# A YOCO-style decoder trunk on one core: rounding of activations at the entry of the recurrent stage, the first loads and filling products, and the end of W_o

## The chip, the cores and the metric

The kernel runs on one core of one Trainium2 chip. The metric is the device time of one execution in microseconds (us); the time of a kernel is the median of its runs. Three runs of the kernel before gave 1004.2, 1003.19 and 1003.34 us, median 1003.34 us.

## The reference, cut to what matters

256 tokens of width 1024 pass through two layers. Layer 0: a SwiGLU feed-forward (half step), a recurrent block (RG-LRU), a second feed-forward. Then keys, values and forget gates are computed once. Layer 1: feed-forward, attention, feed-forward. Every sub-layer has an RMSNorm before and after it. Cut down:

```
def swiglu(x, w_gate, w_up, w_down):
    return (silu(x @ w_gate) * (x @ w_up)) @ w_down

for layer in range(2):
    f = swiglu(rms_norm(h, ffn1_pre_g[layer]), ffn1 weights);  h = h + 0.5 * rms_norm(f, ffn1_post_g[layer])
    hn = rms_norm(h, mix_pre_g[layer])
    m = recurrent_block(hn, ...) if layer == 0 else forgetting_attention(hn, ...)
    h = h + rms_norm(m, mix_post_g[layer])
    f = swiglu(rms_norm(h, ffn2_pre_g[layer]), ffn2 weights);  h = h + 0.5 * rms_norm(f, ffn2_post_g[layer])
```

The recurrent block begins with `gx = x @ w_in` (1024 to 2 x 1344 columns), the attention ends with `o @ w_o`. All is float32.

## The kernel before, in words

**Products.** A float32 product is made of three products of rounded halves (`mm3`, L180 to L185): x and w are each split into an upper part (fp32r, `xhi`, `whi`) and a lower part (`xlo`, `wlo`, the remainder), and upper x upper, upper x lower, lower x upper are accumulated in PSUM. The activations, transposed, are the stationary side; 512 columns of weights stream.

**Tokens.** The 256 tokens are two halves, t=0 and t=1, of 128 rows. The weights stream from HBM in units of up to 128 x 1024 values (512 KB, tile `raw`, five buffers). `split` (L163) makes `whi` on ACT (L175) and `wlo` on DVE (L177), nine buffers each. A unit is used first for t=0, some slots later for t=1; one `slot` is the six products of one unit for one half. So a buffer comes free when t=1 is through with it.

**Order.** TensorE's order (PE) is written by hand: slots follow each other, and `defer(n, fn)` puts a piece of PE work n slots later. ACT, DVE and the DMA queues get their order from a scheduler with costs and priorities, except in the entry (below) and where an instruction is kept in program order. Engines take their instructions strictly in that order.

**Entry of the kernel** (L1083 to L1194, order by hand on all engines). x and the first four weight units are loaded in small pieces by one queue, SP: x's first half `h0` in pieces 0:2, 2:4, 4:8 (of 128 columns each), `h1` in 0:4, 4:8, the weights w0 and w1 in two halves each, w2 and w3 whole. In the text, h0[0:2] is such a piece and w0b the second half of w0. PE first runs filling products on a zeroed tile (`keep_busy`, L123), transposes the gains and x's tiles (`turn`), ACT rounds tile by tile straight from PSUM with the gain as scale (`x_up`), DVE makes the lower part (`x_lo`), and `products(t, i, "0uu ...")` runs the 512-column products of unit i: the digit is the half of the unit, the letters say which part of w and of x.

**Entry of the recurrent stage.** When the down projection of a half is finished, `enter` takes the sums of squares (ACT, L205), 1/rms on GpSimd (POOL, L198 and L200), and adds to h (DVE, L255 and L260). For the recurrent stage alone (`normed_x`) h is normalised again: squares of h in two pieces (ACT), 1/rms (POOL), `hn` (DVE, L285); five slots later PE transposes `hn` (L292), and `to_x` makes x: `xg = transposed * gain` (DVE, L222), `xhi` (ACT, L223), `xlo` (DVE, L228), each over 512 values. In the stage, eight units of the gate weights (called g0 to g7 here) are used for t=0 first, then for t=1.

**W_o.** `row_items` (L412) runs a projection with two PSUM banks per half. The last `rows` units of a half are kept back and run bank by bank, so that bank 0 ends before bank 1 and its squares can start. For t=0 of W_o that means: slot 7 of 8 (k=6) issues nothing on PE, slot 8 issues twelve products. The attention steps of t=1 (logits, exp on ACT, transposes, values) lie between these slots.

Of the kernel before, what the change touches and what calls it, by code (L numbers as in the profile page):

```python
# [9 lines left out]
F32 = mybir.dt.float32  # L10
F32R = mybir.dt.float32r
BF16 = mybir.dt.bfloat16
# [4 lines left out]
P = 128  # L17
D = 1024
# [26 lines left out]
def trunk_kernel(ctx: ExitStack, tc: tile.TileContext, A: dict, out: bass.AP):  # L45
# [19 lines left out]
    def gtbank():  # L65
        return psum.tile([P, 512], F32, tag="gt", name=nm("gt"), bufs=2)
# [14 lines left out]
    def defer(n, fn):  # L81
        pend.append([n, fn])
# [22 lines left out]

    h = [hpool.tile([P, D], F32, tag=f"h{t}", name=f"h{t}") for t in range(2)]

    def load_h(t, a, b):

        nc.sync.dma_start(h[t][:, a * P:b * P], A["x"][0, t * P:(t + 1) * P, a * P:b * P])  # L110
# [3 lines left out]
    idle = spool.tile([P, D], BF16, tag="junk", name="idle", bufs=1)  # L114
    nc.vector.memset(idle[:, :512], 0.0)
# [7 lines left out]
    def keep_busy(n):  # L123

        ps = trbank()
        for _ in range(n):
            nc.tensor.matmul(ps, idle[:, :P], idle[:, :512], start=True, stop=True)

    gT = cpool.tile([P, 56], F32, name="gT")

# [14 lines left out]
    def main_dest(gi, t):  # L145
        return (gi, xhi[:, :, t * P:(t + 1) * P], xlo[:, :, t * P:(t + 1) * P])
# [19 lines left out]
    def split(rawv, parts, n, pieces=1, dve=False):  # L166
        u = Unit()
        hi = wpool.tile([P, 1024], F32R, tag="whi", name=nm("whi"), bufs=WB)
        lo = wpool.tile([P, 1024], F32R, tag="wlo", name=nm("wlo"), bufs=WB)
        m = n // pieces  # L170
        for c in range(0, n, m):
            if dve:
                nc.vector.tensor_copy(hi[:parts, c:c + m], rawv[:, c:c + m])
            else:
                nc.scalar.activation(hi[:parts, c:c + m], rawv[:, c:c + m], AF.Copy)  # L175
            low = nc.gpsimd if dve else nc.vector
            low.tensor_tensor(lo[:parts, c:c + m], rawv[:, c:c + m], hi[:parts, c:c + m].bitcast(F32), ALU.subtract)  # L177
        u.hi, u.lo = hi[:parts, :n], lo[:parts, :n]
        return u
# [57 lines left out]
    rs = [None, None]  # L237

    def stat(t):
        ss = new_ss()  # L240
# [3 lines left out]
    def enter(t, dests, pf, gb, half, last=False, normed=False):  # L244

        f = 1.0 / 16 if half else 1.0 / 32
        ss = new_ss()
        t1 = []
        urgent = tc.high_priority()
        urgent.__enter__()  # L250
        for n in range(2):
            square_sum(pf[n], ss[:, n:n + 1], f)
        for n in range(2):
            t1.append(hpool.tile([P, 512], F32, tag="t1", name=nm("t1"), bufs=2))
            nc.vector.tensor_tensor(t1[n], pf[n], gb[:, n * 512:(n + 1) * 512], ALU.mult)  # L255
        r = rstd_of(ss, 2, f)
        m = 256 if last else 512
        for c in range(0, D, m):
            hn = h[t][:, c:c + m]
            nc.vector.scalar_tensor_tensor(hn, t1[c // 512][:, c % 512:c % 512 + m], r[:, 0:1], hn, ALU.mult, ALU.add)  # L260
            if last:
                nc.sync.dma_start(out[0, t * P:(t + 1) * P, c:c + m], hn)
        urgent.__exit__(None, None, None)
        if last:
            return

        def inputs():
            tps = [to_tp(h[t], n) for n in range(2)]
            for dest in dests:
                to_x(tps, dest)  # L270
            stat(t)

        def norm():
            with tc.high_priority():
                normed_x()

        def normed_x():
            ss = new_ss()
            for n in range(2):
                square_sum(h[t][:, n * 512:(n + 1) * 512], ss[:, n:n + 1])  # L280
            rs[t] = rstd_of(ss, 2)
            hn = []
            for n in range(2):
                hn.append(hpool.tile([P, 512], F32, tag="t1", name=nm("hn"), bufs=2))
                nc.vector.tensor_scalar(hn[n], h[t][:, n * 512:(n + 1) * 512], rs[t][:, 0:1], None, ALU.mult)  # L285

            def go():
                tps = []
                for n in range(2):
                    tp = gtbank()  # L290
                    for j in range(4):
                        nc.tensor.transpose(tp[:, j * P:(j + 1) * P], hn[n][:, j * P:(j + 1) * P], ident)  # L292
                    tps.append(tp)
                to_x(tps, dests[0])
            defer(5, go)

        if normed:
            norm()
        else:
            defer(3, inputs)  # L300

# [110 lines left out]
    def row_items(w, widths, get_x, post, rows=2, dve=False):  # L412

        acc = {}
        kept = [[], []]
        nk = len(widths)
        r0 = 0
        for k, kp in enumerate(widths):  # L420
            def prep(kp=kp, r0=r0, k=k):
                return split(load_raw(w[r0:r0 + kp, :], kp, D), kp, D, dve=dve and k % 2 == 1)

            def work(t, u, k=k):
                if k == 0:
                    acc[t] = [mmbank(), mmbank()]
                m = rows if t == 1 else min(rows, 2)
                if k >= nk - m:
                    kept[t].append((k, u))
                    if k < nk - 1:  # L430
                        return
                    todo = [(kk, uu, n) for n in range(2) for (kk, uu) in kept[t]]
                else:
                    todo = [(k, u, n) for n in range(2)]
                for (kk, uu, n) in todo:
                    mm3(acc[t][n], *get_x(t, kk), uu.hi[:, n * 512:(n + 1) * 512], uu.lo[:, n * 512:(n + 1) * 512],
                        kk == 0, kk == nk - 1)
                if k == nk - 1:
                    post(t, acc[t])
            items.append((prep, work))  # L440
            r0 += kp
# [624 lines left out]
    row_items(A["attn_w_o"][0], [P] * 8, lambda t, k: (att["oh"][t][:, k, :], att["ol"][t][:, k, :]),  # L1066
              lambda t, accs: enter(t, [main_dest(GI[("ffn2", 1)], t)], accs, gbox["mix1"], False), dve=True)
    ahead(n_q + 2, load_gb("mix1", A["mix_post_g"][1]))
    n_att = len(items)

# [13 lines left out]
    begin.__enter__()  # L1084
    raws = [new_raw() for _ in range(OPEN)]

    def load_w(i, a, b):

        nc.sync.dma_start(raws[i][:, a * 512:b * 512].rearrange("p (k n) -> p k n", k=b - a),
                          A["ffn1_w_gate"][0, (2 * i + a) * P:(2 * i + b) * P, :512].rearrange("(k p) n -> p k n", p=P))  # L1090
# [24 lines left out]

    tps = {}

    def turn(t, a, b):

        n = a // 4  # L1120
        if (t, n) not in tps:
            tps[t, n] = gtbank()
        for k in range(a, b):
            nc.tensor.transpose(tps[t, n][:, k % 4 * P:(k % 4 + 1) * P], h[t][:, k * P:(k + 1) * P], ident)

    def x_up(t, a, b):
        for k in range(a, b):
            nc.scalar.activation(xhi[:, k, t * P:(t + 1) * P], tps[t, k // 4][:, k % 4 * P:(k % 4 + 1) * P], AF.Copy,
                                 scale=gT[:, k:k + 1])

    def x_lo(t, a, b):
        for k in range(a, b):
            nc.vector.scalar_tensor_tensor(xlo[:, k, t * P:(t + 1) * P], tps[t, k // 4][:, k % 4 * P:(k % 4 + 1) * P],
                                           gT[:, k:k + 1], xhi[:, k, t * P:(t + 1) * P].bitcast(F32),
                                           ALU.mult, ALU.subtract)

    def products(t, i, order):

        for c in order.split():
# [3 lines left out]
            nc.tensor.matmul(first_acc[t], main_x(t, k)[c[2] == "l"], parts[i][c[1] == "l"][:, j * 512:(j + 1) * 512],  # L1143
                             start=k == 0 and c[1:] == "uu", stop=k == 7 and c == order.split()[-1])

    first_acc.extend(mmbank() for _ in range(2))
# [24 lines left out]
    x_up(1, 2, 4)  # L1171
    w_lo(1, 1, 2)
    products(0, 1, "0uu 0lu 1uu 0ul 1ul")
    turn(0, 4, 8)
# [6 lines left out]
    turn(1, 4, 8)  # L1181
    x_lo(0, 4, 8)
    products(0, 2, "0uu 1uu 0lu 1lu 0ul 1ul")
    x_up(1, 4, 8)
# [108 lines left out]
```

## Time and profile before

| | |
|---|---|
| runs of the kernel | 1004.2, 1003.19, 1003.34 us; median 1003.34 us |
| the profiled execution | 1004.31 us |
| its span, first to last instruction | 1002.6 us, so 1.71 us lie around it |
| mean granted TensorE clock | 0.999 |
| busy time | PE 993.2, weight loads 830.3, DVE 614.2, ACT 530.6, POOL 59.4 us |
| data moved | 178.88 MB, mean 178 GB/s |

The page gives busy time by engine, the span in 40 slices, and the chain of work that ended last. The timeline lists instructions in order of time: start in us, duration in us, engine, line, operation, output and input tiles, count, and in brackets the idle time of the engine before it and what released it. Matmuls are pipelined: the step from one start to the next, not the duration, is what one costs. PEld is the load of the stationary side, SPq and ACTq are the issuing of DMAs by the sequencers of SP and ACT.

### The profile page before, as it was taken

To read this page: it belongs to the slowest core of one execution; us is meant where nothing else is said; L and a number is where in the kernel's file an instruction comes from. 1 tells how busy PE (TensorE), PEld (TensorE's weight loads), DVE (VectorE), ACT (ScalarE), POOL (GpSimd) and SP (SyncE) were. 2 spreads that over 40 slices of the span, in tenths; PEclk is the share of its full clock that TensorE was granted. 3 is DMA by queue.
4 is the path that set the end of the run, shared out by engine and by line. 5 is a ranking of instruction groups with operands and counts; after the bars stand their busy time and mean duration, and the time that the engine had idled before them with its cause. 6 is when DMAs were issued, how large, how long until landed. Compare 5 with 4: busy or idle time off the path is not lost.

```text
span 1002.6 us, 12917 instructions
## 1 busy us (share of the span) xinstructions
PE 993.2 (99%) x4790; PEld 830.3 (83%) x4790; DVE 614.2 (61%) x768; ACT 530.6 (53%) x737; POOL 59.4 (6%) x98
## 2 busy tenths in 40 slices
PE   9999999999999999999999999999999999999997
PEld 6888888889988888888898888888888888888885
DVE  6656554668998555554686655554487475555542
ACT  6645443559986544443564444444466565444431
POOL 2400000100004000000100000000033000000000
PEclk9999999999999999999999999999999999999999
DMA  7867555565336766555467566555554067665531
GB/s 275 297 207 205 189 189 188 166 180 154 109 108 223 215 183 190 188 189 189 123 209 231 177 189 188 182 180 191 162 170 168 7 204 210 189 188 189 188 106 42
DMA packets 92788, 178.88 MB, mean 178 GB/s; under 512 B 11982, under 2 KB 32886, under 8 KB 92726
## 3 DMA queue, kind: packets, MB, share of 16 engines
q1 hardware_dynamic: 91862, 177.94, 55.9%
q8 instruction: 37, 0.61, 0.3%
q0 software_dynamic: 832, 0.12, 0.1%
q14 instruction: 25, 0.20, 0.1%
q10 hardware_dynamic: 32, 0.01, 0.0%
HBM read 176.95 MB, written 1.05 MB: 178 GB/s over the span
## 4 chain that ended last, share of the span: by engine, by line
PE 97%; DVE 1%; ACT 1%; issue 1%; POOL 0%; POOLq 0%; DVEq 0%; ACTq 0%
PE mm L183 28%; PE mm L185 28%; PE mm L184 28%; PE tr L481 2%; PE gt L709 2%; PE mm L1143 1%; PE mm L1027 1%; PE gt L1000 1%; PE mm L190 1%; PE mm L192 1%; PE mm L191 1%; PE gt L214 1%; PE tr L1016 1%; ACT junk L205 0%; PE tr L896 0%
## 5 line engine op out<-in xcount | busy, mean ns | idle before, releaser
L177 DVE TENSOR_TENSOR wlo<-raw,whi 128x1024 fp32r<-128x1024 f32 (+4 forms) x325 | 391.7, 1210 | 270.9 <-ACT whi L175 269.0
L175 ACT ACTIVATE whi<-raw 128x1024 fp32r<-128x1024 f32 (+4 forms) x325 | 338.1, 1045 | 315.6 <-PE mm L185 253.3
L183 PE MATMUL mm<-whi,xhi 128*128 128x512 f32 (+2 forms) x768 | 304.2, 396 | 0.0
L185 PE MATMUL mm<-whi,xlo 128*128 128x512 f32 (+2 forms) x768 | 298.7, 389 | 0.0
L184 PE MATMUL mm<-wlo,xhi 128*128 128x512 f32 (+2 forms) x768 | 298.0, 388 | 0.0
L185 PEld LDWEIGHTS mm<-whi,xlo 128*128 128x128 f32 x768 | 144.2, 188 | 30.5 <-DVE xlo L228 0.3
L184 PEld LDWEIGHTS mm<-wlo,xhi 128*128 128x128 f32 x768 | 144.5, 188 | 28.0 <-DVE wlo L177 0.3
L183 PEld LDWEIGHTS mm<-whi,xhi 128*128 128x128 f32 x768 | 144.3, 188 | 27.5
L183 PE MATMUL mm<-whi,hhi 128*128 128x512 f32 x352 | 139.1, 395 | 0.0
L185 PE MATMUL mm<-whi,hlo 128*128 128x512 f32 x352 | 137.8, 391 | 0.0
L184 PE MATMUL mm<-wlo,hhi 128*128 128x512 f32 x352 | 136.9, 389 | 0.0
L185 PEld LDWEIGHTS mm<-whi,hlo 128*128 128x128 f32 x352 | 66.1, 188 | 15.0
L184 PEld LDWEIGHTS mm<-wlo,hhi 128*128 128x128 f32 x352 | 66.1, 188 | 14.1
L183 PEld LDWEIGHTS mm<-whi,hhi 128*128 128x128 f32 x352 | 66.2, 188 | 13.0
L198 POOL TENSOR_SCALAR nv<-ss 128x1 f32<-128x1 f32 x24 | 12.0, 501 | 884.7 <-ACT junk L205 884.7
L475 DVE SCALAR_TENSOR_TENSOR prod<-mm,rstd,sil 128x512 f32<-128x512 f32 (+1 forms) x48 | 33.9, 706 | 38.0 <-PE mm L185 34.3
L466 ACT ACTIVATE sil<-mm,rstd 128x512 f32<-128x512 f32 (+1 forms) x48 | 31.2, 651 | 40.7 <-PE mm L185 40.7
L485 ACT ACTIVATE hhi<-tr 128x512 fp32r<-128x512 f32 (+1 forms) x48 | 26.6, 555 | 16.0 <-PE tr L481 15.9
L255 DVE TENSOR_TENSOR t<-mm,gb 128x512 f32<-128x512 f32 x24 | 16.3, 689 | 28.7 <-ACT junk L205 28.7
L205 ACT ACTIVATE junk<-mm 128x512 bf16<-128x512 f32 x24 | 14.2, 591 | 32.8 <-PE mm L185 32.8
L486 DVE TENSOR_TENSOR hlo<-tr,hhi 128x512 fp32r<-128x512 f32 (+1 forms) x48 | 30.5, 642 | 1.4
L183 PE MATMUL mm<-whi,zhi 128*128 128x340 f32 (+2 forms) x80 | 28.3, 354 | 0.0
(187 smaller groups left out, 935.6 us busy)
## 6 DMA issues: line engine op xcount, KB each, us to landing
raw<-in_ffn_w_down_dram SPq DMA_DIRECT2D x88, 512.0 KB
raw<-in_ffn_w_up_dram SPq DMA_DIRECT2D x80, 512.0 KB
raw<-in_ffn_w_gate_dram SPq DMA_DIRECT2D x78, 512.0 KB
raw<-in_rg_w_in_dram SPq DMA_DIRECT2D x20, 504.0 KB
raw<-in_ffn_w_gate_dram SPq DMA_DIRECT2D x20, 256.0 KB
raw<-in_rg_w_out_dram SPq DMA_DIRECT2D x10, 504.0 KB
raw<-in_ffn_w_up_dram SPq DMA_DIRECT2D x16, 256.0 KB
raw<-in_w_kv_dram SPq DMA_DIRECT2D x8, 512.0 KB
```

The costliest lines, as they stand in the source:

```text
L175: nc.scalar.activation(hi[:parts, c:c + m], rawv[:, c:c + m], AF.Copy)
L177: low.tensor_tensor(lo[:parts, c:c + m], rawv[:, c:c + m], hi[:parts, c:c + m].bitcast(F32), ALU.subtract)
L183: nc.tensor.matmul(ps, xh, wh, start=first, stop=False)
L184: nc.tensor.matmul(ps, xh, wl, start=False, stop=False)
L185: nc.tensor.matmul(ps, xl, wh, start=False, stop=last)
L255: nc.vector.tensor_tensor(t1[n], pf[n], gb[:, n * 512:(n + 1) * 512], ALU.mult)
L466: nc.scalar.activation(s[:, :nn], ps, AF.Silu, scale=rs[t][:, 0:1])
L475: nc.vector.scalar_tensor_tensor(pr[:, :nn], ps, rs[t][:, 0:1], s, ALU.mult, ALU.mult)
L481: nc.tensor.transpose(tp[:, j * P:(j + 1) * P], pr[:, j * P:(j + 1) * P], ident)
L485: nc.scalar.activation(hv, tp[:, :nn], AF.Copy)
L486: nc.vector.tensor_tensor(lv, tp[:, :nn], hv.bitcast(F32), ALU.subtract)
L709: nc.tensor.matmul(ps[:w, j * S:(j + 1) * S], wv[:, o:o + w], xc[:w, k, :], start=k == 0, stop=k == m - 1)
```

## The change

The entry: the second half of w0, `h1[0:4]` and the second half of w1 are issued on ACT's queue instead of SP's. The filling products read a constant tile that exists before the kernel starts, not a tile that DVE zeroes first; there are six and three of them instead of five and two. The first two tiles of x go to two PSUM banks, the others to banks of other kinds. In the order, `1uu` is put ahead of `0lu`, and the transposes of h0[2:4] go from before `0lu` to after `1lu`.

The entry of the recurrent stage: the transposes come six slots after `norm` instead of five. `to_x_tiles` takes x per 128-column tile straight from PSUM: eight ACT instructions with the gain as scale, eight DVE instructions, instead of two each of L222, L223 and L228. The first `whi` that is split after `norm` is kept in program order (`settled`), and so comes after the squares of h on ACT.

The end of W_o, t=0: one unit is kept back instead of two (`rows0=1`), so slot k=6 has its six products and slot k=7 six. For t=1, and for all other users of `row_items`, nothing changes.

```
     def keep_busy(n):
         for _ in range(n):
-            nc.tensor.matmul(ps, idle[:, :P], idle[:, :512], start=True, stop=True)
+            nc.tensor.matmul(ps, nc.const_aps.tensor(1.0, (P, P), BF16), nc.const_aps.tensor(1.0, (P, 512), BF16),
+                             start=True, stop=True)
...
-                nc.scalar.activation(hi[:parts, c:c + m], rawv[:, c:c + m], AF.Copy)
+                up = nc.scalar.activation(hi[:parts, c:c + m], rawv[:, c:c + m], AF.Copy)
+                if settled[0]:
+                    tc.keep_in_program_order(up)
+                    settled[0] = False
...
+    def to_x_tiles(tps, dest):
+        gi, xh, xl = dest
+        def operands(k):
+            return tps[k // 4][:, k % 4 * P:(k % 4 + 1) * P], gT[:, gi + k:gi + k + 1]
+        with tc.high_priority():
+            for k in range(8):
+                src, g = operands(k)
+                nc.scalar.activation(xh[:, k, :], src, AF.Copy, scale=g)
+            for k in range(8):
+                src, g = operands(k)
+                nc.vector.scalar_tensor_tensor(xl[:, k, :], src, g, xh[:, k, :].bitcast(F32), ALU.mult, ALU.subtract)
...
-                to_x(tps, dests[0])
-            defer(5, go)
+                to_x_tiles(tps, dests[0])
+            defer(6, go)
...
-                m = rows if t == 1 else min(rows, 2)
+                m = rows if t == 1 else rows0
...
     load_h(0, 0, 2)
     load_w(0, 0, 1)
+    load_w(0, 1, 2, nc.scalar)
     load_h(0, 2, 4)
-    load_w(0, 1, 2)
-    load_h(1, 0, 4)
+    load_h(1, 0, 4, nc.scalar)
     load_w(1, 0, 1)
-    load_w(1, 1, 2)
+    load_w(1, 1, 2, nc.scalar)
...
-    keep_busy(5)
+    keep_busy(6)
     gains_T(grow0, 16, 0)
-    turn(0, 0, 2)
-    keep_busy(2)
+    turn(0, 0, 1, gtbank())
+    turn(0, 1, 2, gtbank())
+    keep_busy(3)
...
-    products(0, 0, "0uu 0ul")
-    turn(0, 2, 4)
-    products(0, 0, "0lu 1uu 1ul")
-    turn(1, 0, 4)
+    products(0, 0, "0uu 0ul 1uu 0lu 1ul")
+    turn(1, 0, 2, early[0])
+    turn(1, 2, 4, trbank())
     products(0, 0, "1lu")
+    turn(0, 2, 4, early[1])
```

In the changed program's order, ACT's queue holds: the load of the gains, the table load, one small activation, then the three new loads. The third of them, w1's second half, waits for the semaphore of h0[0:2]. At the entry of the recurrent stage DVE's order for t=0 is: the two additions to h, both `hn`, five `wlo` (L177), four `xlo`, one product with the gain of t=1 (L255), three `xlo`, L255, the two additions to h of t=1, the last `xlo`. ACT's order there is: two squares of the sum, two squares of h, five `whi`, eight `xhi`.

More of the change, by code (lines that the diff above doesn't have):

```diff
@@ L1116, in trunk_kernel, with turn @@
     tps = {}
[L1118 to L1122, printed above, removed]
+    def turn(t, a, b, bank):
         for k in range(a, b):
-            nc.tensor.transpose(tps[t, n][:, k % 4 * P:(k % 4 + 1) * P], h[t][:, k * P:(k + 1) * P], ident)
+            tps[t, k] = bank[:, (k - a) * P:(k - a + 1) * P]
+            nc.tensor.transpose(tps[t, k], h[t][:, k * P:(k + 1) * P], ident)
     def x_up(t, a, b):
         for k in range(a, b):
-            nc.scalar.activation(xhi[:, k, t * P:(t + 1) * P], tps[t, k // 4][:, k % 4 * P:(k % 4 + 1) * P], AF.Copy,
+            nc.scalar.activation(xhi[:, k, t * P:(t + 1) * P], tps[t, k], AF.Copy,
                                  scale=gT[:, k:k + 1])
@@ L1144, in products @@
                              start=k == 0 and c[1:] == "uu", stop=k == 7 and c == order.split()[-1])
+    early = [mmbank() for _ in range(2)]
     first_acc.extend(mmbank() for _ in range(2))
-    keep_busy(5)
+    keep_busy(6)
     gains_T(grow0, 16, 0)
-    turn(0, 0, 2)
-    keep_busy(2)
+    turn(0, 0, 1, gtbank())
+    turn(0, 1, 2, gtbank())
+    keep_busy(3)
     x_up(0, 0, 2)
```

22 lines of the change are left out of this document (11 added, 11 removed).

## Prediction

> **What bounds the kernel now.** I read the page first, then the waits of the weight-load side of TensorE, then the timeline at the three places that the change touches. From the page:
>
> ```profile
> span 1002.6 us, 12917 instructions
> PE 993.2 (99%) x4790; PEld 830.3 (83%) x4790; DVE 614.2 (61%) x768; ACT 530.6 (53%) x737; POOL 59.4 (6%) x98
> PE 97%; DVE 1%; ACT 1%; issue 1%; POOL 0%; POOLq 0%; DVEq 0%; ACTq 0%
> ```
>
> PE is the chain from end to end. The change takes no product away (it adds two fillers), so it can only win where PE stands still or runs slowly. Where it stands still, the waits of its weight loads say (total us, times, longest):
>
> ```profile
> PEld mm L1143 <- ACT xhi L1128: 1.0, 2, 0.5
> PEld mm L1027 <- ACT pT L1018: 0.8, 2, 0.5
> PEld gt L292 <- DVE hn L285: 0.6, 1, 0.6
> ```
>
> L1143 is the entry, L292 the entry of the recurrent stage, L1027 the attention beside W_o. These three are among the longest of that view and hold 2.4 us. So the whole question is about 2 to 4 us in 1003, and 0.2% (2.0 us) is about what a measurement of this kernel can tell from no change.
>
> **A. Entry.** The rows of the stretch:
>
> ```profile
> 0.92 0.27 DVE L115 MEMSET idle<- 128x256 uint32 x1 [0.92 <-PEq L1278]
> 1.24 1.28 ACT L121 ACT_TABLE_LOAD   x1 [1.24 <-PEq L1278]
> 1.25 2.32 PE L127 MATMUL tr<-idle 128*128 128x512 bf16 x5 [1.25 <-DVE idle L115]
> 2.17 0.43 SPq L1089 DMA_DIRECT2D raw<-in_ffn_w_gate_dram  x1
> 2.65 0.43 SPq L110 DMA_DIRECT2D h<-in_x_dram  x1
> 6.34 0.63 ACT L1110 ACTIVATE whi<-raw 128x512 fp32r<-128x512 f32 x1 [1.28 <-DMA raw<-in_ffn_w_gate_dram]
> 7.27 0.63 PE L1143 MATMUL mm<-whi,xhi 128*128 128x512 f32 x1
> 7.70 0.63 PE L1143 MATMUL mm<-whi,xlo 128*128 128x512 f32 x1
> 8.00 0.78 PEld L1124 LDWEIGHTS gt<-ident,h 128*128 128x128 f32 x4 [0.39 <-DMA h<-in_x_dram]
> 10.51 0.40 PE L1143 MATMUL mm<-whi,xhi 128*128 128x512 f32 x1
> 10.74 0.40 PE L1143 MATMUL mm<-wlo,xhi 128*128 128x512 f32 x1
> 4.80:10.20 5.40, 4.41 (x7) 2.33 (x8) 1.00 0.89 312
> ```
>
> Two things cost here. First the pitch: products start 0.43 us apart at 7.27 and 7.70, 0.23 apart at 10.51 and 10.74, although the last row (L1143 alone: busy time and count of products on PE and of their weight loads, then granted clock, DMA share, GB/s) shows the granted clock at 1.00. It has seven products in 5.4 us. At the later pitch they would take 7 x 0.23 = 1.6; the slow pitch costs 7 x 0.20 = 1.4, and the rest, 2.4, is transposes and waiting for loads: w0b until 6.34, `h1[0:4]` until 8.00, then its rounding.
>
> The loads: w0b's issue moves from 2.17 to about 1.25 if ACT's queue goes on beside the table load, or back to 2.5 (1.24 + 1.28) if it waits for that; `h1[0:4]` from 2.65 to 1.7, or 3.0. Bounds for the gain of `h1[0:4]`: 0.95 us if issuing sets it, below nothing (-0.5) if ACT's queue is late. w0b was used 4.2 us after its issue and `h1[0:4]` 5.3 after, so each waits for others' bytes; I take half, 0.5 us. That `xhi` now needs only the first two transposes of t=1 saves two at 0.2 (four load in 0.78 at 8.00); the two of h0[2:4], now ahead of t=1's products, cost the same. The third filler costs nothing as long as PE waits for w0b behind it (0.43 if it doesn't). So 0.5.
>
> The pitch: fillers start when PE does, not behind DVE's 0.27 us memset, 0.3 us earlier, and nine of them instead of seven reach without a gap to about 5.5. If denser work brings the faster pitch sooner, each product ahead of 10.2 wins 0.20. Bounds: 0 (it changes at the same time) and 1.4 (all seven); the waits for loads take the place of most of it, so I take 0.3. **A = -0.8, from +0.5 (ACT's queue late) to -2.0 (0.95 and three quarters of 1.4).** Nothing behind eats it: from 10.2 to 20.7 ACT is busy 8.8 and DVE 9.0 of 10.5 us, so up to 1.5 us pass through.
>
> ```profile
> 10.20:20.70 10.50, 10.50 (x50) 8.45 (x49) 9.03 (x20) 8.78 (x19) 0.30 (x1) 1.00 0.82 286
> 17.25 2.02 ACT L175 ACTIVATE whi<-raw 128x1024 fp32r<-128x1024 f32 x2
> ```
>
> SP's load of the fifth unit now waits for w1's first half instead of w0b, so it is issued later; ACT rounds that unit at 17.25, which hides it.
>
> **B. Entry of the recurrent stage.**
>
> ```profile
> 185.62 0.30 POOL L198 TENSOR_SCALAR nv<-ss 128x1 f32<-128x1 f32 x1 [147.85 <-ACT junk L205]
> 188.09 1.03 ACT L175 ACTIVATE whi<-raw 128x1008 fp32r<-128x1008 f32 x1
> 189.03 0.61 ACT L205 ACTIVATE junk<-h 128x512 bf16<-128x512 f32 x1
> 189.83 0.70 POOL L198 TENSOR_SCALAR nv<-ss 128x1 f32<-128x1 f32 x1 [3.25 <-ACT junk L205]
> 191.15 0.39 PE L185 MATMUL mm<-whi,hlo 128*128 128x512 f32 x1
> 191.21 0.88 DVE L285 TENSOR_SCALAR hn<-h,rstd 128x512 f32<-128x512 f32 x2 [0.84 <-POOL rstd L200]
> 191.75 1.09 PE L292 MATMUL gt<-ident,hn 128*128 128x128 f32 x8 [0.22 <-DVE hn L285]
> 192.60 0.47 PE L183 MATMUL mm<-whi,hhi 128*128 128x512 f32 x1
> 196.81 0.39 PE L183 MATMUL mm<-whi,xhi 128*128 128x504 f32 x1
> 197.30 0.50 PE L185 MATMUL mm<-whi,xlo 128*128 128x504 f32 x1
> 203.58 0.40 PE L185 MATMUL mm<-whi,xlo 128*128 128x504 f32 x1
> 204.44 1.06 PE L292 MATMUL gt<-ident,hn 128*128 128x128 f32 x8 [0.47 <-DVE hn L285]
> 205.26 0.47 PE L183 MATMUL mm<-whi,xhi 128*128 128x504 f32 x1
> 801.14 0.39 PE L185 MATMUL mm<-whi,ol 128*128 128x512 f32 x1
> 802.16 0.48 PE L183 MATMUL mm<-whi,oh 128*128 128x512 f32 x1
> ```
>
> Between the last two rows lie eight transposes without a wait (L214): 1.02 us from the product before to the product after. Here it is 191.15 to 192.60 = 1.45 and 203.58 to 205.26 = 1.68: 0.43 and 0.66 us of standstill. A first `xlo` that comes late (197.30: 0.50 instead of 0.39) adds 0.11. Together 1.2.
>
> After: without the `whi` of 188.09 ahead of it the second square starts with its h, near 188.1, instead of 189.03. POOL's first step starts 0.8 later (189.83), and lasts 0.30 as at 185.62, not 0.70, as no `wlo` is running on DVE; `hn` starts 0.68 after its end: 189.9, ending 190.8. The transposes come six products (1.37 us) later, at 191.38 + 1.37 = 192.75. Both waits go. What is late next is DVE: five `wlo` now stand between `hn` and the first `xlo`. At 1.18 each (192.00 has two in 2.32) they end at 190.8 + 5.9 = 196.7; `xlo` of a tile takes 0.285 (14.40 has four in 1.13), ready at 196.95. PE goes on at 193.55, has twelve products until 196.3 and wants that `xlo` two products on, at 196.75: a new wait of 0.2, longer by whatever `hn` is late. `xhi` is no limit: five `whi` from 188.85, some 1.03 each, end at 194.0, and the tiles follow at 0.285 (13.22 has four in 1.14). The last `xlo` stands behind h of t=1: 0.1 more. **B = -1.2 + 0.3 = -0.9**; from -1.2 (no new wait) to 0 (the new wait as long as the old ones).
>
> ```profile
> 192.00 2.32 DVE L177 TENSOR_TENSOR wlo<-raw,whi 128x1008 fp32r<-128x1008 f32 x2
> 13.22 1.14 ACT L1128 ACTIVATE xhi<-gt,gT 128x128 fp32r<-128x128 f32 x4 [0.67 <-PE gt L1124]
> 14.40 1.13 DVE L1133 SCALAR_TENSOR_TENSOR xlo<-gt,gT,xhi 128x128 fp32r<-128x128 f32 x4 [0.54 <-ACT xhi L1128]
> ```
>
> **C. W_o.**
>
> ```profile
> 789.53 0.60 PE L1039 MATMUL tr<-ident,ot 128*128 128x128 f32 x4
> 790.44 1.10 PE L1027 MATMUL mm<-v,pT 128*128 128x64 f32 x8 [0.31 <-ACT pT L1018]
> ```
>
> Eight transposes took 0.8 above (1.02 less a product), so these four take 0.4 and the values could follow at 789.93; they wait for `pT` until 790.44: 0.5 us. After, six products (1.37 us) stand between and cover it. The first product behind transposes lasts 0.47 (192.60) instead of 0.39, and one such start is added: 0.1. The step after keeps six products between its transposes and its values, as all other steps have, and none of those waits. The sum of bank 0 ends 3 instead of 6 products before the slot's end, but the whole slot is 0.6 earlier. **C = -0.4**, from -0.6 to 0.
>
> **Sum.** -0.8 - 0.9 - 0.4 = -2.1. Against the profiled execution's own 1004.31 (span 1002.6 and 1.71 around it) that is 1002.2; that execution stands 0.97 above the median of the runs, which I carry over: 1003.34 - 2.1 = **1001.2**, 0.21% less.
>
> **Rivals.**
>
> 1. *The second queue moves only the issuing.* For: the data moved at 312 GB/s with the DMA engines 0.89 busy between 4.8 and 10.2, and w0b took 4.2 us from issue to use. Against: the first microseconds are not full. Then w0b and `h1[0:4]` land when they did, the third filler and the reordered transposes show, and A is +0.1 instead of -0.8: -1.2, **1002.1**. The Trainium skill, "DMA: Bandwidth & Descriptors", section "Issuing engines are not separate DMA queues", says just this: DMAs started by several engines run on the same 16 DMA engines and interleave, and starting them from several saves only the sequencer's time. By that rule this rival is the forecast.
> 2. *The pitch changes early.* If denser fillers bring the 0.23 us pitch at about 6.8 and loads come 0.95 earlier too, A is -2.0: -3.3, **1000.0**. For: the runs of the same kernel differ by 1.0 us, as much as five products' slow pitch. Against: the profile before had seven fillers and still changed its pitch only between 7.70 and 10.51. The Trainium skill, "TensorE: Matmul & The Clock Gate", Part 1, "What's actually happening", has the array at half clock until a free-running window of about 3.4 us was busy; the two pitches agree with it, the granted clock of 1.00 does not show it.
> 3. *DVE's five `wlo` cost what was won*: if `hn` ends at 191.7 instead of 190.8, as late as before less 0.4, the first `xlo` is 1.1 us late and B is 0: -1.2, **1002.1**. For: DVE takes its instructions in order and stands idle until `hn`. Against: the two squares lose the `whi` between them, which alone is 0.9.
> 4. *Slower: ACT's queue starts after the table load.* w0b lands after 6.9, PE stands still behind the fillers for over 1 us, and the faster pitch comes only after the products of unit 1 and the first six of unit 2: 18 x 0.20 = 3.6, and 0.4 for the loads. A is +4.0: +2.7, **1006.0**. It decides from w0b landing later than 6.9. Against: the queue of a sequencer and its engine are shown apart in the trace.
> 5. *The change doesn't do what it says*: in the changed order the waits' causes are in fact moved, so I give this no case of its own; C at 0 is within the range.
>
> **How the numbers follow.** Forecast 0.42, own range 1000.5 to 1002.0; rival 1 0.24, rival 2 0.18, rival 3 0.10, rival 4 0.06. The boundary of 0.2% is 1001.33, just above the forecast, which so gives 0.27 to faster and 0.15 to same; rival 2 is faster; rivals 1 and 3 are same but for 0.03; rival 4 is slower. Faster 0.48, same 0.46, slower 0.06. The range goes from 999.8 to 1002.9: rivals 1 to 3 with half a microsecond around them.
>
> **What would show it.** A: ACTq issues near 1.25, w0b's `whi` before 6.34, the 0.23 pitch before 10. B: no idle time before the transposes of `hn`; a PE wait of 0.2 to 0.3 on `xlo` at the first product of g0. C: no wait on `pT` there. The prediction is wrong if the products of unit 1 start later than before, or if PE waits more than 1 us on `xlo`.

## The result and the profile after

| | before | after |
|---|---|---|
| median of the runs | 1003.29 us (17 runs, 1002.9 to 1004.2) | 1001.38 us (17 runs, 1000.82 to 1002.81) |
| the profiled execution | 1004.31 us | 1001.1 us |
| ratio after to before | | 0.998, 95% interval 0.9972 to 0.9987 |

The changed kernel is 1.9 us faster at the median, the forecast was 1001.2. The two profiled executions differ by more, 3.2 us; that difference turns out to be the main point below.

The page after. PE is still the chain from end to end, and is busy 2.2 us less than before:

```profile
span 999.4 us, 12928 instructions
PE 991.0 (99%) x4792; PEld 829.4 (83%) x4792; DVE 613.0 (61%) x775; ACT 532.7 (53%) x749; POOL 59.0 (6%) x98
```

The waits of its weight loads (total us, times, longest). The rows of before for `xhi` at the entry (1.0), `hn` (0.6) and the longer one for `pT` are gone; what is left of B is one wait of a weight load for `xlo` (0.3, of which the products lose 0.1, as the rows of B show). The wait for `pT` that is left was there before, as the shorter of two:

```profile
PEld mm L187 <- DVE xlo L251: 0.3, 1, 0.3
PEld mm L1045 <- ACT pT L1036: 0.3, 1, 0.3
```

**A.** The timeline of the entry after. Both queues issue side by side, ACT's beside the table load. But w0a, which was rounded at 4.18 before, comes at 5.63, and PE stands still for it; from the second product on, though, products start 0.23 apart unless PE waits or transposes between them:

```profile
1.24 1.28 ACT L119 ACT_TABLE_LOAD   x1 [1.24 <-PEq L1296]
1.31 0.37 ACTq L1107 DMA_DIRECT2D raw<-in_ffn_w_gate_dram  x1
...
5.63 0.43 DVE L1126 CAST whi<-raw 128x512 fp32r<-128x512 f32 x1 [1.65 <-DMA raw<-in_ffn_w_gate_dram]
5.82 0.63 ACT L1128 ACTIVATE whi<-raw 128x512 fp32r<-128x512 f32 x1 [0.98 <-DMA raw<-in_ffn_w_gate_dram]
...
6.20 0.47 PE L1159 MATMUL mm<-whi,xhi 128*128 128x512 f32 x1 [0.57 <-DVE whi L1126]
6.51 0.39 PE L1159 MATMUL mm<-whi,xlo 128*128 128x512 f32 x1
...
19.26 0.40 PE L185 MATMUL mm<-whi,xhi 128*128 128x512 f32 x1
```

The same rows of before, w0a's rounding, the first product and the first regular product:

```profile
4.18 0.43 DVE L1108 CAST whi<-raw 128x512 fp32r<-128x512 f32 x1 [0.19 <-DMA raw<-in_ffn_w_gate_dram]
4.85 0.82 PE L1143 MATMUL mm<-whi,xhi 128*128 128x512 f32 x1
20.72 0.39 PE L183 MATMUL mm<-whi,xhi 128*128 128x512 f32 x1
```

The first regular product is the first one behind the hand-ordered entry. The busy times of the entry's products alone from 4.8 to 10.2 (PE, weight loads, granted clock, DMA share, GB/s) hold fourteen products where before held seven:

```profile
4.80:10.20 5.40, 3.80 (x14) 2.50 (x14) 1.00 1.01 362
```

**B.** The eight transposes of `hn` follow the products without a wait, for both halves; only the first product with `xlo` is stretched, 0.33 us to the next start instead of 0.23:

```profile
188.56 0.88 DVE L302 TENSOR_SCALAR hn<-h,rstd 128x512 f32<-128x512 f32 x2 [1.99 <-POOL rstd L202]
189.36 5.68 DVE L179 TENSOR_TENSOR wlo<-raw,whi 128x1008 fp32r<-128x1008 f32 x5
191.28 1.04 PE L309 MATMUL gt<-ident,hn 128*128 128x128 f32 x8
195.36 0.49 PE L187 MATMUL mm<-whi,xlo 128*128 128x504 f32 x1
195.69 0.39 PE L185 MATMUL mm<-whi,xhi 128*128 128x504 f32 x1
203.25 1.04 PE L309 MATMUL gt<-ident,hn 128*128 128x128 f32 x8
222.28 3.62 PE L727 MATMUL gt<-xc,gw 126*126 126x256 f32 x16
```

**C.** Six products stand between the transposes of `ot` and the values, which no longer wait:

```profile
786.96 0.60 PE L1057 MATMUL tr<-ident,ot 128*128 128x128 f32 x4
787.31 0.48 PE L185 MATMUL mm<-whi,oh 128*128 128x512 f32 x1
...
788.79 1.00 PE L1045 MATMUL mm<-v,pT 128*128 128x64 f32 x8
992.00 0.40 PE L187 MATMUL mm<-whi,hlo 128*128 128x512 f32 x1
```

The last row is the last product of the kernel. Between such fixed points the time can be split: the first regular product (end of the entry), the first gate product `gt<-xc,gw` (222.28 here), the transposes of `ot` (786.96), the last product. Before they stood at 20.72, 224.86, 789.53 and 995.21:

```profile
224.86 3.62 PE L709 MATMUL gt<-xc,gw 126*126 126x256 f32 x16
995.21 0.40 PE L185 MATMUL mm<-whi,hlo 128*128 128x512 f32 x1
```

Every later table uses these four; the stretches are called A, B and C after the part of the change that lies in them.

| us | before | after | difference |
|---|---|---|---|
| up to the first regular product (A) | 20.72 | 19.26 | -1.46 |
| from there to the first gate product (B) | 204.14 | 203.02 | -1.12 |
| from there to the transposes of `ot` | 564.67 | 564.68 | 0 |
| from there to the last product (C) | 205.68 | 205.04 | -0.64 |

### The profile page after: what moved, and what is told of

Its sections match the earlier page's. It is cut to its first block, busy times and chain, and to the rows that moved or that the text cites. A ratio compares the mean times of both kernels' runs of the same rounds, so it can differ in the third digit from the quotient of the medians.

```text
span 999.4 us, 12928 instructions
## 1 busy us (share of the span) xinstructions
PE 991.0 (99%) x4792; PEld 829.4 (83%) x4792; DVE 613.0 (61%) x775; ACT 532.7 (53%) x749; POOL 59.0 (6%) x98
## 4 chain that ended last, share of the span: by engine, by line
PE 99%; DMA 0%; DVE 0%; POOLq 0%; ACT 0%; issue 0%; DVEq 0%; SPq 0%; POOL 0%; ACTq 0%
PE mm L185 29%; PE mm L187 29%; PE mm L186 29%; PE tr L499 2%; PE gt L727 2%; PE mm L1159 1%; PE gt L1018 1%; PE mm L192 1%; PE mm L194 1%; PE mm L1045 1%; PE mm L193 1%; PE gt L216 1%; PE tr L1034 1%; DMA raw<-in_ffn_w_gate_dram 0%; PE tr L914 0%; PE tr L796 0%
```

## Experiments: each part alone

Four kernels: the new entry alone, the new stage entry alone, the new end of W_o alone, and the last two together.

**The entry alone.** B and C undone in the changed kernel:

```
-                to_x_tiles(tps, dests[0])
-            defer(6, go)
+                to_x(tps, dests[0])
+            defer(5, go)
-            settled[0] = True
-                m = rows if t == 1 else rows0
+                m = rows if t == 1 else min(rows, 2)
```

> This has the new entry alone: the first loads by two queues, the fillers on the stored constant, the transposes turned two by two; the entry of the recurrent stage and W_o are those of before. Theory 1 (the profiled execution of before is one of its late ones): the profile after reached the first regular product 1.46 us earlier than the profile before, but the medians of both kernels differ only by 1.91 us, and B and C took 1.13 and 0.56 of that in the profiles. So the median here is only 0.2 us below that of the kernel before (0 to 0.5), whatever the profiles say. Theory 2 (the gain of the profiles is there in every execution): the median is 1.5 us below. Both expect the first product of unit 0 near 6.2, w0a landing near 5.6 and the pitch of 0.23 from the first product on.

Measured 1003.42 us (11 runs) against 1003.41 (33 runs), ratio 0.9999 (0.999 to 1.0008). So the entry by itself brings nothing that the whole time shows; the 1.5 us of theory 2 is excluded, and the 0.2 of theory 1 lies inside the interval. The span says a little more: its median is 1001.4 us, against 1001.7 in the runs of before taken with it, while the time around the span is 1.93 us instead of 1.72 at the median. Why this kernel has more time around its span is not known. Its own first regular product stood at 19.88.

**The stage entry alone.** Into the kernel before:

```
-                to_x(tps, dests[0])
-            defer(5, go)
+                to_x_tiles(tps, dests[0])
+            defer(6, go)
+            settled[0] = True
```

> The new entry of the recurrent stage alone; entry and W_o are those of before. Theory 1: from the first regular product to the first gate product of the recurrent stage it takes 1.1 us less than before, as in the profile after (202.95-203.05 against 204.14), and the median falls by 1.1 us. Rival: part of those 1.1 us came from the new entry (another phase of DVE and ACT when the stage starts), and this stretch shrinks by less than 0.8 alone. The entry, which is that of before, shows by its own profile whether the products' pitch changes between 7.7 and 10.5 again or at once: theory 1 expects executions of both kinds.

**W_o alone.** `rows0=1` into the kernel before:

```
-                m = rows if t == 1 else min(rows, 2)
+                m = rows if t == 1 else rows0
```

> The new end of W_o alone. Theory 1: 0.56 us between the last gate product's stretch and the last product, as in the profile after, because the wait of the values on pT goes (0.5) and the next step's transposes have no wait; the median falls by 0.5. Rival: half of the 0.56 is the restart behind transposes moved elsewhere, and the median falls by 0.3 or less. Entry as before: the first regular product near 20.7 or near 19.7, by when the pitch changes.

**Both, with the entry of before.**

> The change without its entry: the entry of the recurrent stage and W_o's end are new, the first loads, fillers and transposes are those of before. Theory 1 (the new entry brings 0.2 us at the median): 1.7 us below the kernel before, 1001.6, hardly above the changed kernel's 1001.4. Theory 2 (the new entry brings the 1.46 us that the profiles show): 0.5 us below the kernel before, since 1.9 in all less 1.46 is left, 1002.8. Parts are independent if this run's gain is that of the new stage entry alone plus that of W_o alone within 0.2.

Medians of 11 runs each, and the stretches of the profiles:

| | median, us | ratio to before | first regular product | B stretch | C stretch |
|---|---|---|---|---|---|
| A alone | 1003.42 | 0.9999 (0.999 to 1.0008) | 19.88 | 204.12 | 205.68 |
| B alone | 1002.62 | 0.9991 (0.9982 to 1.0) | 20.11 | 202.98 | 205.68 |
| C alone | 1002.84 | 0.9997 (0.9988 to 1.0005) | 19.61 | 204.14 | 205.06 |
| B and C | 1002.06 | 0.9985 (0.9976 to 0.9994) | 19.62 | 203.07 | 205.05 |

B is worth 1.07 to 1.16 us wherever it is, C 0.62 to 0.64, and neither needs the others. The medians alone (-0.8, -0.6, and -1.35 for both) say the same less sharply. Against what was expected: B alone fell by 0.8 and not 1.1 in the median, though its stretch did; C alone as theory 1 had it; both together fell by as much as the two gains added, so the parts are independent, but 1.35 lies between theory 1 (1.7) and theory 2 (0.5), nearer to the first. Part of what the medians miss lies outside these stretches: behind the last product the profiles of B alone and of both take 7.55 and 7.60 us, all other profiles 7.33 to 7.40; the cause is open. The stretch between B and C is 564.65 to 564.68 in all of them. What differs is the first column: three kernels with the very same entry as before have their first regular product at 20.11, 19.61 and 19.62, not at 20.72. Their timelines show one reason. The entry of C alone has the slow pitch only until 7.27:

```profile
7.27 0.43 PE L1161 MATMUL mm<-whi,xhi 128*128 128x512 f32 x1
7.53 0.39 PE L1161 MATMUL mm<-whi,xlo 128*128 128x512 f32 x1
19.61 0.39 PE L186 MATMUL mm<-whi,xhi 128*128 128x512 f32 x1
```

From 7.27 on starts are 0.26 and 0.23 apart, where the profile of before still had 0.43 at 7.70 and did not reach 0.23 until 10.51. So the date at which the pitch changes is not a property of the kernel: it varies between executions, and the profiled execution of before was one with a late date. The loads vary too: B alone has the quick pitch earlier than C alone, yet ends its entry 0.5 us later, as its transposes of `h1[0:4]` start at 8.19 after a wait of 0.46 us for that load, those of C alone at 7.76 without one.

Since stretches that an edit leaves alone repeat within about 0.1 us in nearly all profiles (up to 0.25 behind the last product), each run's time tells its own first regular product: profiled first regular product plus run time less profiled run time (an estimate). Over the 109 runs of the kernel before it lies between 19.25 and 21.69, median 19.73, 16 of them above 20.4. With the new entry (the changed kernel and the entry alone, 28 runs) it lies between 18.98 and 20.97, median 19.55, one above 20.4. So **A is worth about 0.2 us at the median**, not the 1.46 of the two profiles. The direct comparisons, from 0 (the entry alone against before) to 0.7 (the changed kernel against B and C, taken side by side with different runs of before), lie around it and are no sharper. With an error of some 0.2 us in the estimate itself, A is small, and its size is not known better than that.

The second queue also makes the end of the entry depend on a load that is wanted later. With the entry of after, w1b is rounded at 9.62 to 10.43 in the four profiles with the quick pitch, each time after a wait for the load; PE then stands still up to 1.17 us for it. In the run with five units of the section on the stage entry, the pitch is quick from the first product at 5.61 on, and the first regular product still comes only at 20.07:

```profile
10.42 0.63 ACT L1128 ACTIVATE whi<-raw 128x512 fp32r<-128x512 f32 x1 [1.73 <-DMA raw<-in_ffn_w_gate_dram]
11.10 0.50 PE L1159 MATMUL mm<-whi,xhi 128*128 128x512 f32 x1 [1.17 <-ACT whi L1128]
```

So a late end of the entry can come from the slow pitch or from a late load, and the estimate from a run's time does not tell them apart.

## Experiments: inside the entry

**All first loads by SP, in the order of before.**

```
-    load_w(0, 1, 2, nc.scalar)
     load_h(0, 2, 4)
-    load_h(1, 0, 4, nc.scalar)
+    load_w(0, 1, 2)
+    load_h(1, 0, 4)
     load_w(1, 0, 1)
-    load_w(1, 1, 2, nc.scalar)
+    load_w(1, 1, 2)
```

> The changed kernel with all first loads issued by SP in the order of before. Theory 1 (the two queues share the bytes: w0b's and h1's early issue takes from w0a what it gives to w0b): w0a lands near 4.2 again instead of 5.6 and the first product starts near 4.9 instead of 6.2, w0b lands after 6.3 again, and the first regular product comes within 0.2 us of the changed kernel's 19.55 at the median. Rival (h1[0:4] earlier by the second queue is the gain of the entry): the first regular product comes 0.3 us later, 19.85, where the old entry is.

1001.56 us (11 runs); first regular product at the median 19.78. w0a is rounded at 4.65 and w0b at 6.50, so PE starts early and then waits 1.2 us for w0b, which the new order of the products wants as the third:

```profile
4.65 0.43 DVE L1126 CAST whi<-raw 128x512 fp32r<-128x512 f32 x1 [0.67 <-DMA raw<-in_ffn_w_gate_dram]
...
7.18 0.50 PE L1159 MATMUL mm<-whi,xhi 128*128 128x512 f32 x1 [1.19 <-ACT whi L1128]
```

The second queue gave w0b 0.7 us and took 1.0 from w0a. All profiles bear this out: w0a is rounded at 4.01 to 4.65 in the seven with one queue and at 4.97 to 5.92 in the seven with two; w0b, with the loads in the order of before or of after, at 6.32 to 6.55 and 5.18 to 6.12. As theory 1 expected the two nearly cancel; the 0.2 that remains lies at the edge of both theories.

**One queue, in the order of use.** h0[2:4], whose transposes the change moved back, goes behind h1[0:4]:

```
     load_w(0, 0, 1)
-    load_h(0, 2, 4)
     load_w(0, 1, 2)
     load_h(1, 0, 4)
+    load_h(0, 2, 4)
```

> The changed kernel with all first loads issued by SP, and h0[2:4] behind h1[0:4], in the order in which the new order of the transposes uses them. Theory (the entry is bound by when the bytes for the first six products of each tile come, in their order of use): w0a lands near 4.2, w0b near 5.9 and h1[0:4] near 7.5, so PE starts at 4.9 and stands less behind it; the first regular product at 19.2 at the median, 0.3 below the changed kernel, 1001.0. Rival (the products before the pitch changes, near 6 to 7, cost twice, which eats the early start): no difference, 19.5.

**1000.29 us** (7 runs, 1000.05 to 1000.72), ratio to before 0.9972 (0.996 to 0.9983): its slowest run is faster than the fastest of the changed kernel (1000.82; the runs of before taken beside each of the two have the same median, 1003.29), and it gains more than the theory asked: first regular product 18.44 in the profile, 18.5 at the median, no run above 18.93. Both halves of w0 are there before the fillers end (the first fence, the timeline), and seventeen products fit into the stretch that held seven before and fourteen after (the second, the same busy times as above):

```profile
4.19 0.43 DVE L1126 CAST whi<-raw 128x512 fp32r<-128x512 f32 x1 [0.21 <-DMA raw<-in_ffn_w_gate_dram]
4.95 0.63 ACT L1128 ACTIVATE whi<-raw 128x512 fp32r<-128x512 f32 x1
5.10 0.98 PE L1159 MATMUL mm<-whi,xhi 128*128 128x512 f32 x1
```

```profile
4.80:10.20 5.40, 4.90 (x17) 3.43 (x17) 1.00 0.93 312
```

**Fillers of before** in the changed kernel:

```
+    nc.vector.memset(idle[:, :512], 0.0)
-            nc.tensor.matmul(ps, nc.const_aps.tensor(1.0, (P, P), BF16), nc.const_aps.tensor(1.0, (P, 512), BF16),
-                             start=True, stop=True)
+            nc.tensor.matmul(ps, idle[:, :P], idle[:, :512], start=True, stop=True)
-    keep_busy(6)
+    keep_busy(5)
-    keep_busy(3)
+    keep_busy(2)
```

> The changed kernel with the fillers of before: five and two on a tile that DVE zeroes first. Theory (PE busy 0.4 us earlier and without a gap until 5.6 is what makes every execution of the new entry enter its products at the 0.23 us pitch): here some executions show the 0.43 pitch in the first products again, and the first regular product's spread over the executions grows from 0.9 to over 1.2 us, its median by 0.2 to 0.4. Rival (the fillers do nothing; the loads or the order of the transposes do): median and spread as in the changed kernel, 19.55.

1002.13 us (11 runs); first regular product at the median 20.19, and above 20.4 in five of 11 runs. The profiled execution is one of these, though its first product is earlier than after's:

```profile
5.54 0.77 PE L1160 MATMUL mm<-whi,xhi 128*128 128x512 f32 x1
6.10 0.63 PE L1160 MATMUL mm<-whi,xlo 128*128 128x512 f32 x1
...
10.30 0.39 PE L1160 MATMUL mm<-whi,xhi 128*128 128x512 f32 x1
```

In the five kernels with the whole new entry (the changed kernel, the entry alone, and the three of the next section) 8 of 61 runs are above 20.4, but from none to four of 11 in a single kernel; of the kernel before, 16 of 109 are. With the fillers of before the median grew by 0.65 us and the spread to 1.95 us, both by more than the theory had it, so the fillers may make a late end rarer. That they do so through the pitch is not shown, since a run's time doesn't tell a late pitch from a late load; and they don't exclude the late pitch, as the run without the kept order shows.

**The order of use with w0b and w1b on ACT's queue.**

```
     load_w(0, 1, 2, nc.scalar)
-    load_h(0, 2, 4)
-    load_h(1, 0, 4, nc.scalar)
+    load_h(1, 0, 4)
+    load_h(0, 2, 4)
```

> The loads' order of use (h0[0:2], w0a, w0b, h1[0:4], h0[2:4], w1) as in the run with one queue that had its first regular product at 18.5, but w0b and w1b issued by ACT at 1.31 and after. Theory 1 (the order of the bytes decides, not who issues): w0a lands within 0.3 us of 4.2 and the first regular product at 18.5 at the median. Theory 2 (loads started side by side share the bytes, so a second queue delays w0a): w0a lands near 5 or later, the first product starts half a microsecond or more later than 5.1, and the first regular product is at 18.9 to 19.5.

1000.88 us (11 runs), in two groups: six runs with a first regular product of 18.7 to 19.1, five of 20.4 to 21.1. w0a is rounded at 5.04 instead of 4.19, and the gains too come later (PE stands still for `grow`, 0.26 us in the midst of the fillers):

```profile
1.31 0.85 ACTq L1107 DMA_DIRECT2D raw<-in_ffn_w_gate_dram  x2
3.81 0.26 PE L132 MATMUL tr<-ident,grow 16*128 16x16 f32 x1 [0.26 <-DMA grow<-in_ffn_pre_g_dram]
5.04 0.43 DVE L1126 CAST whi<-raw 128x512 fp32r<-128x512 f32 x1 [0.76 <-DMA raw<-in_ffn_w_gate_dram]
```

Theory 2 holds: loads started side by side delay the one that is wanted first. Order of use brings more than the queue (19.54 to 19.08 with two queues, 19.78 to 18.5 with one), but with two queues only in about half of the runs; what makes the other five late was not seen, as the profile is one of the early six. With one queue every run keeps the gain.

**One filler less** in the best kernel (`keep_busy(2)` ahead of the first product).

> The kernel with one queue in the order of use, with two instead of three fillers ahead of the first product. Theory (the third filler, 0.43 us, stands ahead of products whose inputs are there at 4.8): the first product starts 0.3 us earlier, and the first regular product at 18.2 at the median, 1000.0. Rival (the products just before the pitch changes cost twice, or PE then stands still for w0b): 18.5 again, with more spread.

1000.41 us (8 runs). The profiled execution has its first product at 4.67 and its first regular one at 18.22, as the theory has it; over the runs the median is 18.64, the spread 18.2 to 19.4. The rival holds: what the earlier start wins does not last to the end of the entry at the median. The profile, one of the early runs, has the slow pitch between its first two products (4.67 and 5.10).

## Experiments: inside the stage entry

**Without the kept order of `whi`.**

```
         if normed:
             norm()
-            settled[0] = True
```

> The changed kernel without the one line that keeps the first whi of the recurrent stage in program order; the rest of the new stage entry stays. Theory (the whi of 1.03 us between the two squares is what made hn late): a whi stands between the squares again, hn ends about 0.9 us later and its transposes wait 0.2 us or more; the stretch from the first regular to the first gate product grows from 203.0 us by 0.2 to 0.6. Rival (six products more ahead of the transposes hide it all): the stretch stays within 0.1 of 203.0.

1001.72 us (11 runs); B stretch 203.06, so the rival holds. A `whi` does stand between the squares again, POOL's step lasts 0.70 again, and `hn` ends 1.2 us later measured from the first regular product. Nobody waits for it:

```profile
188.24 1.03 ACT L174 ACTIVATE whi<-raw 128x1008 fp32r<-128x1008 f32 x1
189.98 0.70 POOL L200 TENSOR_SCALAR nv<-ss 128x1 f32<-128x1 f32 x1 [3.25 <-ACT junk L207]
191.36 0.88 DVE L302 TENSOR_SCALAR hn<-h,rstd 128x512 f32<-128x512 f32 x2 [0.85 <-POOL rstd L202]
192.88 1.03 PE L309 MATMUL gt<-ident,hn 128*128 128x128 f32 x8
```

**Five units instead of six** (`defer(5, go)`).

> The changed kernel with the transposes of hn five instead of six units of products behind, as before; everything else is new. The run without the kept order of whi showed hn ending 1.2 us later and still no wait, so the kept order alone could not be what took the waits away. Theory (the sixth unit alone covers both waits, and the kept order covers the first as well): at t=0 no wait (hn ends near 189.4, the transposes come at 191.3 less 1.4), at t=1 the wait is back, and the stretch from the first regular to the first gate product is 203.0 plus 0.4 to 0.7. Rival (both are needed): both waits are back, 204.1. Rival 2 (neither, the tile by tile rounding took them away): 203.0.

1002.34 us (11 runs); B stretch 203.71, 0.69 more than after: the theory holds, at the upper end of its 0.4 to 0.7. At t=0 the transposes have no wait; at t=1 they wait, and a second wait appears (the product with `xlo` at 200.63 starts 0.52 us after the one before it), as the last two `xlo` now fall behind h of t=1 on DVE:

```profile
190.68 1.03 PE L309 MATMUL gt<-ident,hn 128*128 128x128 f32 x8
200.22 0.60 DVE L251 SCALAR_TENSOR_TENSOR xlo<-gt,gT,xhi 128x128 fp32r<-128x128 f32 x2
200.63 0.50 PE L187 MATMUL mm<-whi,xlo 128*128 128x504 f32 x1
203.34 1.10 PE L309 MATMUL gt<-ident,hn 128*128 128x128 f32 x8 [0.15 <-DVE hn L302]
```

**The rounding of before behind six units** (`to_x` in place of `to_x_tiles`).

> The changed kernel with the rounding of before in the entry of the recurrent stage (four tiles at a time through a product with the gain) behind the six units. Theory (the tile by tile rounding is a reserve, as the first xlo was waited for only 0.1 us in both): the stretch from the first regular to the first gate product is 203.0 to 203.3. Rival (the first product of g0 would wait for a whole bank's xlo, behind five wlo on DVE): PE waits 0.5 us or more at each tile's first product with xlo, and the stretch is 203.6 or more.

1003.35 us (11 runs), no faster than the kernel before (1003.33); B stretch 204.49, 1.5 more than after: the theory fell, the rival holds. `xhi` of four tiles needs `xg` from DVE first, which stands behind four `wlo`; ACT then waits for DVE, and PE for both:

```profile
194.55 1.28 DVE L224 TENSOR_TENSOR xg<-gt,gT 128x512 f32<-128x512 f32 x2
195.96 0.61 ACT L225 ACTIVATE xhi<-xg 128x512 fp32r<-128x512 f32 x1
196.62 0.49 PE L185 MATMUL mm<-whi,xhi 128*128 128x504 f32 x1 [0.85 <-ACT xhi L225]
197.61 0.50 PE L187 MATMUL mm<-whi,xlo 128*128 128x504 f32 x1 [0.26 <-DVE xlo L230]
```

So the gain of B needs both six units and the rounding tile by tile: five units with the new rounding keep 0.43 of its 1.12, six units with the old rounding are 0.35 slower than before. The kept order of `whi` is a reserve that nothing uses as long as there are six units; no run leaves it out with five units.

## Why the prediction was right, and where it was not

The forecast of 1001.2 was met (1001.38), but by terms that erred in opposite ways: A won 0.6 less than predicted, B and C together 0.46 more. That the errors cancel is luck.

**A, predicted -0.8, was about -0.2.** The step that failed is "I take half, 0.5 us" for the earlier issue of w0b and `h1[0:4]`. It priced what the second queue brings forward and not what it delays: w0a went from 4.18 to 5.63 and the first product from 4.85 to 6.20, and w1b's load is waited for at the end. Neither the forecast nor rival 1 had that; rival 1, that the queue moves only the issuing, is wrong in its mechanism (w0b came 0.5 earlier) and near in its sum. The Trainium skill, "DMA: Bandwidth & Descriptors", section "Issuing engines are not separate DMA queues", says that such loads interleave on the same DMA engines; the runs agree (w0a rounded at 4.19 with one queue, 5.04 with two, in the same order of use). That all they save is issuing time is too kind here: in these two profiles they cost the first load 0.85 us.

**Rival 2 named the right mechanism and gave it to the wrong side.** The pitch did change before the first product, and the two profiles differ by most of the price that it named (-1.46 of the -2.0). But the executions of before mostly change it earlier too: the three other profiles of that entry have the quick pitch by about 6 to 7.3, and by the estimate above 93 of the 109 runs of before end their entry at 20.4 or below. The prediction took the pitch change between 7.70 and 10.51 as a fact about the kernel, where it was one about the execution. Its own hint, that "the runs of the same kernel differ by 1.0 us, as much as five products' slow pitch", pointed at it, though loads that come late are part of that spread. Carrying over the 0.97 us between the profiled execution and the median as a constant was the same error: other profiles with that entry end it 0.6 to 1.1 us earlier, so most of the 0.97 lies in the entry, and a gain measured against it is partly counted twice. The Trainium skill, "TensorE: Matmul & The Clock Gate", Part 1, "What's actually happening", calls the window free-running and gives this as the reason why the change's date varies, by 0.5 us either way. The dates here do vary, but by much more (by 6.2 in the profile after, at 9.9 in another execution of the same entry), and the granted clock shows none of it.

**B, predicted -0.9, was -1.12.** The waits removed were 1.2 as worked out. From `hn` to the first `xlo` every date came within 0.3 us of the working (laid against the first regular products, 1.46 apart: `hn` ended at 190.9, predicted 190.8; transposes at 192.74, predicted 192.75). The mis-sized term is the new waits: 0.3 predicted, 0.1 measured, since the last `xlo` came in time and the first one 0.1 late. Why the waits go was told only in part: the working took the earlier `hn` and the later transposes together, and worked out t=0 only. The runs show that the later transposes are enough without the earlier `hn`, and that with five units t=1's wait is back. Rival 3's price did not come where its condition was met: without the kept order `hn` ended 1.2 us later, but DVE then had one `wlo` less behind it, and the stretch grew by 0.04 us. What it feared, `wlo` on DVE ahead of what PE wants, appears in another form where the rounding of before is kept, and costs 1.5 us.

**C, predicted -0.4, was -0.64.** The wait on `pT` went as worked out: the step from the `ot` transposes to the values is 0.45 us shorter once the six products between them (1.37) are taken off, and the 0.1 for one more start behind transposes is paid in it. What the sum lacked lies behind: the values themselves take 0.11 less (790.44 to 791.38 before, 788.79 to 789.62 after), and 0.08 goes further on that no single row shows.

**Rival 4** fell at once: ACT's queue issues at 1.31, beside the table load.

## What to carry to other kernels

Order the first loads by their first use on one queue, and look at which other load pays when a second queue is opened: that gave 1.1 us here where the new entry with two queues gave about 0.2. Before a start-up phase of one profiled execution is priced, see how far the runs of that kernel lie apart, since a stretch that varies between executions can't be read from one of them; fixed points further on, between which the profiles agree within 0.1 us, can be compared. When a wait is removed by moving work later, try each part of the edit by itself: here one part did nothing beside the others, and another that looked like polish was needed for the gain.

## What was not expected of the hardware

The products' pitch went from 0.43 to 0.23 us anywhere between about 4 and 10 us in executions of nearly the same entry, with a granted clock of 1.00 recorded throughout. The earliest is the run with the rounding of before, whose three fillers ahead of the first product already start 0.2 us apart (the first row below). The first regular product lay within 2.4 us over the runs of before (19.25 to 21.69, as estimated above); the pitch and the loads both have a part in that, and how much each has was not separated. What fixes the date in one execution was not settled: PE stood still 1.03 us ahead of the first product in the run with the new entry alone and was at the fast pitch, and 0.73 us in the run without the kept order and was at the slow one until 9.9 (the last two rows).

```profile
4.00 0.81 PE L125 MATMUL tr<-const-bfloat16-1.0 128*128 128x512 bf16 x3
...
6.39 0.76 PE L1158 MATMUL mm<-whi,xhi 128*128 128x512 f32 x1 [0.73 <-DVE whi L1125]
9.94 0.44 PE L1139 MATMUL mm<-ident,h 128*128 128x128 f32 x2
```
